# FFN inputs of a two-layer diffusion backbone: scale and shift of the turned tiles in one pass from PSUM, split between ScalarE and VectorE, and the column blocks' sums all on VectorE

## The chip, the cores and the metric

The kernel runs on one core of one Trainium2 chip. The metric is the device time of one execution in microseconds (us); the time given is the median of three runs. The engines are called TensorE (PE in the profile; PEld are its weight loads), VectorE (DVE), ScalarE (ACT), GpSimd (POOL) and SyncE (SP, which issues the DMAs). Each engine works through its own queue in order. TensorE writes its results to PSUM; in this kernel VectorE and ScalarE read them from there, and GpSimd works on SBUF alone.

## The reference

512 latent tokens and 256 context tokens with 1024 features pass through two layers. Each layer has a mixer and then a SwiGLU FFN; the input of each is normalised and modulated. What matters here is the FFN's input and its two first projections:

```python
def rms_norm(x, g):
    xf = x.astype(jnp.float32)
    y = xf * lax.rsqrt(jnp.mean(xf * xf, -1, keepdims=True) + NORM_EPS)
    return (y * g.astype(jnp.float32)).astype(x.dtype)

def modulate(h, shift, scale):
    return h * (1.0 + scale) + shift

def swiglu(u, w_gate, w_up, w_down):
    return (jax.nn.silu(u @ w_gate) * (u @ w_up)) @ w_down

# in each layer, behind the mixer's output y (and yc, the context's, in the first layer):
h = h + gt_m * rms_norm(y, g_post_mix[i])
f = swiglu(modulate(rms_norm(h, g_pre_ffn[i]), sh_f, sc_f), w_ffn_gate[i], w_ffn_up[i], w_ffn_down[i])
```

In the first layer all 768 tokens go through the FFN, in the second only the 512 latent ones. The FFN is 2816 wide.

## The kernel before

**Precision.** Every product of fp32 matrices is made of three products of halves: a value is split into a high part (ScalarE, `hi`) and a rest (`lo`, the value minus its high part, made by VectorE unless the call names GpSimd). This is the helper `split`, lines 179 to 182, so its instructions all bear lines 181 and 182 and are told apart by their tiles. TensorE then does high by high, high by rest and rest by high (`mm3`, lines 196 to 199).

**The output projection and what follows it** (`out_proj`, line 1403). A tile is 128 tokens: six in the first layer, worked on in the order 0 to 5, four in the second, in the order 0, 2, 1, 3. For each tile TensorE makes the second half of the projection (lines 1410 to 1412). ScalarE squares it for the norm (`junk`, line 1451), GpSimd makes the reciprocal root from the sums (`rr`, lines 221 and 228), and VectorE adds the result to the stream (lines 1536 to 1539 in the first layer, 2255 to 2258 in the second). Then `norm_W` (line 1505) prepares the FFN's input: ScalarE squares the new row (line 337), GpSimd makes `rr` again, ScalarE scales the row (`hn`, line 1508). TensorE turns the tile, four 128x128 blocks for each half of the 1024 features, into one of two PSUM banks (`ptp`, line 1513). In the turned tile the features lie on the partitions, so the norm's gain times (1 + scale) and the shift are one number per partition and block of features (`acol`, `scol`). VectorE multiplies the 128x512 half by its gains (line 1516), into the tile `nt`; the shift is added in a second pass (line 1517), by GpSimd for the first half of the features and by VectorE for the second. `Lagged(1)` puts one tile's second part behind the next tile's first part.

**The seven blocks.** The gate and up projections use Strassen's scheme in Winograd's form: a pair of token tiles makes the two columns of a 2x2 block matrix, the halves of the features its two rows, and seven products take the place of eight. `Winograd.add` (line 1485) makes the columns' seven blocks of each pair from the four `nt` halves. An even tile's halves are blocks 0 and 4 as they are. With an odd tile come four differences: block 1 (line 1492), block 2 (line 1497), block 3 (line 1499) and block 6 (line 1502), and block 5 is the tile's second half itself. Each block is split into `ub0` and `ub1` (both called `ub` in the profile) by `put`. Lines 1492 and 1499 are on GpSimd, except for the last tile, where they are on VectorE; line 1502 and the rest of block 5 (line 1501) are on GpSimd; the others are on VectorE.

**The FFN's first products** (`gate_up`, line 1566). For each pair of blocks of the weights and each of the two weight matrices, seven weight blocks meet the seven column blocks. Each product takes one block index of all pairs at once, so block 0 must be there for every pair before the first product can run through. The first two products use the blocks 0 and 4, the next ones 1, 5, 2, 3 and 6. The weights' own sums (`s`, lines 1603 to 1606) are made by GpSimd in the first layer; in the second layer three of four are made by VectorE. The sums of the products (lines 1609 to 1614) are on VectorE, the gate's activation on ScalarE, and the product of gate and up on GpSimd (line 1662).

**What sets the order.** The instructions of each engine are put in order by a planner before the launch, from the order in which the program issues them and from its own estimate of each instruction's time. The program issues a tile's preparation before the FFN's weights, but the planner lets weight work go ahead when it holds that the tile isn't ready.

Of the kernel before, what the change touches and what calls it, by code (L numbers as in the profile page):

```python
# [154 lines left out]
AF = mybir.ActivationFunctionType  # L155
ALU = mybir.AluOpType
# [7 lines left out]
def emit(tc, A):  # L164
    nc = tc.nc
    V, S, G, T = nc.vector, nc.scalar, nc.gpsimd, nc.tensor
# [8 lines left out]
    def bc(ap, n):  # L175

        return ap.unsqueeze(len(ap.shape)).to_broadcast(list(ap.shape) + [n])

    def split(hi, lo, src, lo_eng=None):

        S.activation(hi, src, AF.Copy)  # L181
        (lo_eng or V).tensor_tensor(lo, src, hi.bitcast(F32), ALU.subtract)  # L182
# [36 lines left out]
    def rsqrt_(out, ss, add):  # L219

        G.tensor_scalar(out, ss, add, None, ALU.add)
        n = 1
        for s in out.shape[1:]:
            n *= s
        nh = nhalf[:, :n]
        if len(out.shape) == 3:
            nh = nh.rearrange("p (a b) -> p a b", a=out.shape[1])
        G.tensor_tensor(out, out, nh, ALU.pow)
# [105 lines left out]
    def rstd_of(src, junk):  # L334
        ss = sm.tile([128, 1], F32, tag="ss", name="ss")
        r = sm.tile([128, 1], F32, tag="rr", name="rr")
        S.activation(junk, src, AF.Square, scale=1.0 / 32.0, accum_out=ss)
        rsqrt_(r, ss, EPS)
        return r

    def norm_T(src, a_col, s_col, pst, hi_out, lo_out):

        hn = tmpp.tile([128, 1024], F32, tag="hn", name="hn", bufs=2)
        r = rstd_of(src, hn)
        S.activation(hn, src, AF.Copy, scale=r)
        yield
        for hf in range(2):
            ps = pst()
            for k in range(4):
                T.transpose(ps[:, k * 128:(k + 1) * 128], hn[:, (hf * 4 + k) * 128:(hf * 4 + k + 1) * 128], ident)  # L350
            t = tmpp.tile([128, 4, 128], F32, tag="nt", name="nt", bufs=2)
            V.tensor_tensor(t, ps.rearrange("p (k t) -> p k t", k=4), bc(a_col[:, hf * 4:hf * 4 + 4], 128), ALU.mult)
            G.tensor_tensor(t, t, bc(s_col[:, hf * 4:hf * 4 + 4], 128), ALU.add)
            for (h, l, sv) in zip(hi_out(hf), lo_out(hf), split_view(t, len(hi_out(hf)))):
                split(h, l, sv)

    class Lagged:

# [4 lines left out]
        def add(self, gen):  # L363
            next(gen)
            self.q.append(gen)
            if len(self.q) > self.lag:
                self.pop()
# [22 lines left out]
    def split_view(t, n):  # L390
        if n == 1:
            return [t]
        v = t.rearrange("p k (r b c) -> p k r b c", r=2, b=8)
        return [v[:, :, i] for i in range(2)]
# [36 lines left out]
    def ptp(name="ptp"):  # L431
        return bank("v", name)
# [150 lines left out]
    def stile(nm):  # L583
        return gc.tile([128, 6, 16], F32, name=nm, tag=nm)

    av, gv, bv = stile("av"), stile("gv"), stile("bv")
    t0, t1, t2 = stile("t0"), stile("t1"), stile("t2")
# [26 lines left out]
    for d in range(2):  # L614
        rhs = gv[:, :, d * 8:(d + 1) * 8]
        ps = ptp("cum")
# [5 lines left out]
        ps = ptp("rest")  # L622
# [7 lines left out]
    for p in range(2):  # L630
        ps = ptp("tot")
# [828 lines left out]
    class Winograd:  # L1460
# [24 lines left out]
        def add(self, t, half_, x):  # L1485
            i = t // 2
            if t % 2 == 0:
                self.kept[i, half_] = x
                self.put(i, 4 * half_, x, V)
            elif half_ == 0:  # L1490
                b11 = self.kept[i, 0]
                (V if t == self.last else G).tensor_tensor(b11, x, b11, ALU.subtract)
                self.put(i, 1, b11, V)
                self.kept[i, 2] = x
            else:
                t1, b21, b12 = self.kept[i, 0], self.kept[i, 1], self.kept[i, 2]
                V.tensor_tensor(b12, x, b12, ALU.subtract)
                self.put(i, 2, b12, V)
                (V if t == self.last else G).tensor_tensor(t1, x, t1, ALU.subtract)
                self.put(i, 3, t1, V)  # L1500
                self.put(i, 5, x, G)
                G.tensor_tensor(b21, b21, t1, ALU.subtract)
                self.put(i, 6, b21, V)

    def norm_W(src, a_col, s_col, pst, U, t):
        hn = tmpp.tile([128, 1024], F32, tag="hn", name="hn", bufs=2)
        r = rstd_of(src, hn)
        S.activation(hn, src, AF.Copy, scale=r)
        yield
        for hf in range(2):  # L1510
            ps = pst()
            for k in range(4):
                U.turned = T.transpose(ps[:, k * 128:(k + 1) * 128], hn[:, (hf * 4 + k) * 128:(hf * 4 + k + 1) * 128], ident)
            x = tmpp.tile([128, 4, 128], F32, tag="nt", name="nt", bufs=6)
            ks = slice(hf * 4, hf * 4 + 4)
            V.tensor_tensor(x, ps.rearrange("p (k t) -> p k t", k=4), bc(a_col[:, ks], 128), ALU.mult)
            (V if hf else G).tensor_tensor(x, x, bc(s_col[:, ks], 128), ALU.add)
            U.add(t, hf, x)


# [10 lines left out]
    def post_mix0(t, ps, ss):  # L1531
        v = 0 if t < 4 else 1
        xt = tmpp.tile([128, 1024], F32, tag="xt", name="xt", bufs=2)
        nc.sync.dma_start(xt, A['x'][t * 128:(t + 1) * 128] if t < 4 else A['cx'][(t - 4) * 128:(t - 3) * 128])
        yt = tmpp.tile([128, 512], F32, tag="yt", name="yt")
        V.tensor_tensor(yt, ps, GG[v][:, 512:1024], ALU.mult)
        r = add_rstd(ss)
        V.scalar_tensor_tensor(xt[:, 0:512], U0.spare(t), r, xt[:, 0:512], ALU.mult, ALU.add)
        V.scalar_tensor_tensor(xt[:, 512:1024], yt, r, xt[:, 512:1024], ALU.mult, ALU.add)
        nc.sync.dma_start(h_d[t], xt)  # L1540
        yield from norm_W(xt, acol[v][:, 1, :], scol[v][:, 1, :], ptp, U0, t)
# [295 lines left out]
    def post_ffn0(t):  # L1837
        v = 0 if t < 4 else 1
        yield from norm_T(h[:, t, :], acol[v][:, 2, :], scol[v][:, 2, :], ptp, u_views(u1['h'], t), u_views(u1['l'], t))
# [413 lines left out]
    def post_mix1(t, ps, ss):  # L2253
        t2 = tmpp.tile([128, 512], F32, tag="yt", name="yt")
        V.tensor_tensor(t2, ps, GGs['m1'][0][:, 512:1024], ALU.mult)
        r = add_rstd(ss)
        V.scalar_tensor_tensor(h[:, t, 0:512], U1.spare(t), r, h[:, t, 0:512], ALU.mult, ALU.add)
        V.scalar_tensor_tensor(h[:, t, 512:1024], t2, r, h[:, t, 512:1024], ALU.mult, ALU.add)
        yield from norm_W(h[:, t, :], acol[0][:, 3, :], scol[0][:, 3, :], ptp, U1, t)
# [50 lines left out]
```

## Time and profile before

| | |
|---|---|
| median of three runs | 1999.85 us (1995.31 to 2003.21) |
| the profiled execution | 1996.12 us |
| its span in the profile | 1994.0 us |
| TensorE busy | 1830.4 us, 92% of the span |
| VectorE busy | 1436.1 us, 72% |
| ScalarE busy | 966.6 us, 48% |
| GpSimd busy | 928.0 us, 47% |
| granted TensorE clock, mean | 0.956 of full speed |

The profile comes from one execution. Its parts are the busy time of each engine, the span in 40 slices, the chain of work that ended last, and the groups of instructions by line, engine and tile with their count, busy time, mean duration and the idle time ahead of them. The trace can be asked the same of a stretch of time, and for the waits: which engine stood still at which line until which other engine's instruction had ended. A group's line reads: line, engine, operation, output<-inputs, shape, count; then busy us, mean ns; then the idle time before. Buffer numbers are left out of the names. A duration reaches from an instruction's start to its end; a queued instruction starts a little before its predecessor's end, so that durations in a row overlap slightly.

The changed lines run twice: from about 685 to 740 us (first layer) and from about 1607 to 1645 us (second layer).

### The profile page before, as it was taken

Reading aid. Unit: us, or ns where it says so; the run is one execution under the profiler, and the core shown is the slowest. Engines: PE = TensorE matmul, PEld = TensorE weight load, DVE = VectorE, ACT = ScalarE, POOL = GpSimd, SP = SyncE. Lnnn points to the kernel's source line nnn. Section 1 sums busy time; section 2 is a strip of 40 time slices with the busy share of each in tenths; the row PEclk is TensorE's granted clock in tenths of the full one; section 3 lists DMA queues with packets and bytes.
Section 4 is the critical chain, followed back from the end, with each engine's and each line's share of the span. In section 5 each row is a group of like instructions: output and inputs, shape, how many; then the busy total and the mean of one; then the engine's idle time right before and its main releaser. Section 6 shows DMA issues by size and latency. Waiting matters only on the chain.

```text
span 1994.0 us, 33781 instructions
## 1 busy us (share of the span) xinstructions
PE 1830.4 (92%) x12760; PEld 1504.2 (75%) x12760; DVE 1436.1 (72%) x2040; ACT 966.6 (48%) x1816; POOL 928.0 (47%) x828
## 2 busy tenths in 40 slices
PE   6989978989898979999999998889989959999998
PEld 3877855656566869999997776677655659999886
DVE  3686757677876696666656886887566589999654
ACT  4433457666874553333333345533455445445443
POOL 2387454344533376556547665653256142333101
PEclk7999978888999989999999999999999979999999
DMA  8255694665724613222227543586634212333221
GB/s 305 84 153 149 203 296 129 182 188 155 243 80 141 244 64 106 80 75 75 64 75 258 161 153 101 172 280 207 184 106 121 85 64 85 106 107 96 85 95 64
DMA packets 125751, 280.20 MB, mean 141 GB/s; under 512 B 12882, under 2 KB 43498, under 8 KB 125588
## 3 DMA queue, kind: packets, MB, share of 16 engines
q1 hardware_dynamic: 125588, 278.03, 44.0%
q8 instruction: 101, 1.65, 0.3%
q14 instruction: 62, 0.51, 0.1%
HBM read 226.15 MB, written 46.07 MB: 137 GB/s over the span
## 4 chain that ended last, share of the span: by engine, by line
PE 53%; DVE 9%; issue 4%; DMA 4%; POOL 3%; ACT 3%; SPq 0%; POOLq 0%; DVEq 0%; ACTq 0%
PE st L198 9%; PE st L199 9%; PE st L197 9%; PE dn L1696 4%; PE dn L1697 4%; PE dn L1698 4%; PE po L188 2%; DVE macc L254 2%; DMA mraw<-in_wmb_dram 2%; PE y L1410 1%; PE y L1411 1%; PE y L1412 1%; PE st L1958 1%; DVE ub L182 1%; PE st L1959 1%
## 5 line engine op out<-in xcount | busy, mean ns | idle before, releaser
L197 PE MATMUL st<-ub,hi_gu 128*128 128x384 f32 (+1 forms) x1232 | 385.8, 313 | 22.1 <-ACT ub L181 22.1
L198 PE MATMUL st<-ub,hi_gu 128*128 128x384 f32 (+1 forms) x1232 | 385.6, 313 | 1.1 <-DVE ub L182 1.0
L199 PE MATMUL st<-ub,lo_gu 128*128 128x384 f32 (+1 forms) x1232 | 384.3, 312 | 0.9 <-POOL lo_gu L182 0.9
L197 PEld LDWEIGHTS st<-ub,hi_gu 128*128 128x128 f32 x1232 | 233.9, 190 | 23.0 <-ACT ub L181 23.0
L199 PEld LDWEIGHTS st<-ub,lo_gu 128*128 128x128 f32 x1232 | 234.6, 190 | 1.6 <-POOL lo_gu L182 1.2
L198 PEld LDWEIGHTS st<-ub,hi_gu 128*128 128x128 f32 x1232 | 233.5, 190 | 2.0 <-DVE ub L182 2.0
L181 ACT ACTIVATE hi_gu<-s 128x512 fp32r<-128x512 f32 x176 | 111.1, 631 | 175.1 <-PE st L198 164.4
L1696 PE MATMUL dn<-hi_wd,gh 128*128 128x512 f32 x440 | 175.2, 398 | 2.2 <-ACT gh L181 2.2
L1697 PE MATMUL dn<-lo_wd,gh 128*128 128x512 f32 x440 | 175.0, 398 | 1.8 <-DVE lo_wd L182 1.8
L1698 PE MATMUL dn<-hi_wd,gl 128*128 128x512 f32 x440 | 165.3, 402 | 5.2 <-POOL gl L182 5.2
L182 DVE TENSOR_TENSOR lo_gu<-raw_gu,hi_gu 128x512 fp32r<-128x512 f32 x132 | 129.9, 998 | 42.8 <-ACT hi_gu L181 42.8
L182 DVE TENSOR_TENSOR lo_gu<-s,hi_gu 128x512 fp32r<-128x512 f32 x154 | 128.2, 833 | 45.1 <-ACT hi_gu L181 45.1
L254 DVE SCALAR_TENSOR_TENSOR macc<-mraw,cs,macc 128x1024 f32<-128x1024 f32 x80 | 125.5, 1592 | 22.8 <-DMA mraw<-in_wmb_dram 16.3
L181 ACT ACTIVATE hi_gu<-raw_gu 128x512 fp32r<-128x512 f32 x132 | 82.0, 629 | 98.8 <-PE st L198 91.9
L182 DVE TENSOR_TENSOR lo_wd<-raw_wd,hi_wd 128x512 fp32r<-128x512 f32 x110 | 96.8, 885 | 44.4 <-ACT hi_wd L181 44.3
L1606 POOL TENSOR_TENSOR s<-raw_gu 128x512 f32<-128x512 f32 x44 | 74.4, 1692 | 84.3 <-issue 70.7
L904 ACT ACTIVATE P<-st 128x512 f32<-128x512 f32 x128 | 73.0, 596 | 65.5 <-PE st L199 28.5
L1698 PEld LDWEIGHTS dn<-hi_wd,gl 128*128 128x128 f32 x440 | 82.3, 189 | 28.6 <-POOL gl L182 7.9
L1696 PEld LDWEIGHTS dn<-hi_wd,gh 128*128 128x128 f32 x440 | 83.0, 189 | 24.3 <-ACT gh L181 3.1
L181 ACT ACTIVATE gh<-g 128x512 fp32r<-128x512 f32 x76 | 47.5, 631 | 110.9 <-PE dn L1697 101.8
L1697 PEld LDWEIGHTS dn<-lo_wd,gh 128*128 128x128 f32 x440 | 83.0, 189 | 23.4 <-DVE lo_wd L182 2.7
L1662 POOL TENSOR_TENSOR g<-g,up 128x512 f32<-128x512 f32 x38 | 55.7, 1465 | 86.5 <-DVE up L1611 55.8
(545 smaller groups left out, 4794.7 us busy)
## 6 DMA issues: line engine op xcount, KB each, us to landing
mraw<-in_wmb_dram SPq DMA_DIRECT2D x56, 512.0 KB
raw_wd<-in_wd_dram SPq DMA_DIRECT2D x55, 512.0 KB
raw_gu<-in_wg_dram SPq DMA_DIRECT2D x44, 512.0 KB
raw_gu<-in_wu_dram SPq DMA_DIRECT2D x44, 512.0 KB
cu<-in_wmb_dram SPq DMA_DIRECT2D x24, 512.0 KB
raw_m<-in_wmb_dram SPq DMA_DIRECT2D x16, 512.0 KB
raw_qkv<-in_wqkv_dram SPq DMA_DIRECT2D x12, 512.0 KB
raw_tok<-qk_d SPq DMA_DIRECT2D x12, 512.0 KB
```

Of the source, the lines that this page charges most:

```text
L181: S.activation(hi, src, AF.Copy)
L182: (lo_eng or V).tensor_tensor(lo, src, hi.bitcast(F32), ALU.subtract)
L197: T.matmul(out, wh, xh, start=start, stop=False)
L198: T.matmul(out, wh, xl, start=False, stop=False)
L199: T.matmul(out, wl, xh, start=False, stop=stop)
L254: V.scalar_tensor_tensor(a, raw, cs[:, self.k, v:v + 1], a, ALU.mult, ALU.add)
L904: S.activation(P[:, :n], ps[:, :n], AF.Exp)
L1606: G.tensor_tensor(s3, a11, a21, ALU.subtract)
L1662: G.tensor_tensor(g, g, u, ALU.mult)
L1696: T.matmul(ps, gh[:, tsl], wh, start=start, stop=False)
L1697: T.matmul(ps, gh[:, tsl], wl, start=False, stop=False)
L1698: T.matmul(ps, gl_[:, tsl], wh, start=False, stop=stop)
```

## The change

The pass over a turned half tile becomes four smaller ones, one for each block of 128 features, each doing scale and shift at once from PSUM with the two numbers per partition as operands: by ScalarE for the first half of the features, by VectorE for the second. The separate shift falls away on both engines. The four instructions of `Winograd.add` that were on GpSimd (the differences for the blocks 1, 3 and 6, and the rest of block 5) go to VectorE.

```diff
+    def scaled(x, ps, a_col, s_col, hf):
+
+        for k in range(4):
+            a, b = [c[:, hf * 4 + k:hf * 4 + k + 1] for c in (a_col, s_col)]
+            if hf == 0:
+                S.activation(x[:, k, :], ps[:, k * 128:(k + 1) * 128], AF.Identity, scale=a, bias=b)
+            else:
+                V.tensor_scalar(x[:, k, :], ps[:, k * 128:(k + 1) * 128], a, b, ALU.mult, ALU.add)
...
@@ class Winograd, add
             elif half_ == 0:
                 b11 = self.kept[i, 0]
-                (V if t == self.last else G).tensor_tensor(b11, x, b11, ALU.subtract)
+                V.tensor_tensor(b11, x, b11, ALU.subtract)
                 self.put(i, 1, b11, V)
                 self.kept[i, 2] = x
             else:
                 t1, b21, b12 = self.kept[i, 0], self.kept[i, 1], self.kept[i, 2]
                 V.tensor_tensor(b12, x, b12, ALU.subtract)
                 self.put(i, 2, b12, V)
-                (V if t == self.last else G).tensor_tensor(t1, x, t1, ALU.subtract)
+                V.tensor_tensor(t1, x, t1, ALU.subtract)
                 self.put(i, 3, t1, V)
-                self.put(i, 5, x, G)
-                G.tensor_tensor(b21, b21, t1, ALU.subtract)
+                self.put(i, 5, x, V)
+                V.tensor_tensor(b21, b21, t1, ALU.subtract)
                 self.put(i, 6, b21, V)
...
@@ norm_W
             x = tmpp.tile([128, 4, 128], F32, tag="nt", name="nt", bufs=6)
-            ks = slice(hf * 4, hf * 4 + 4)
-            V.tensor_tensor(x, ps.rearrange("p (k t) -> p k t", k=4), bc(a_col[:, ks], 128), ALU.mult)
-            (V if hf else G).tensor_tensor(x, x, bc(s_col[:, ks], 128), ALU.add)
+            scaled(x, ps, a_col, s_col, hf)
             U.add(t, hf, x)
```

## The prediction

> **What bounds the kernel now.** The changed lines run in two short stretches, behind the output projections of the two layers, before their FFNs. I first asked what TensorE waits for there and afterwards. PE is TensorE, DVE VectorE, ACT ScalarE, POOL GpSimd; each wait row gives total us, times, longest. The waits of TensorE from 694 to 740 us (first layer, six token tiles):
>
> ```profile
> PE st L197 <- ACT ub L181: 5.6, 1, 5.6
> PE ptp L1513 <- DVE nt L1516: 4.3, 1, 4.3
> PE ptp L1513 <- ACT hn L1508: 3.0, 2, 2.2
> ```
>
> From 1607 to 1646 us (second layer, four tiles):
>
> ```profile
> PE st L197 <- ACT ub L181: 16.6, 2, 12.7
> PE ptp L1513 <- ACT hn L1508: 2.5, 1, 2.5
> ```
>
> From 740 to 1000 us, then from 1642 to 1860 us, the FFNs' products:
>
> ```profile
> PE st L199 <- POOL lo_gu L182: 0.9, 1, 0.9
> ```
>
> ```profile
> PE st L198 <- DVE ub L182: 1.0, 1, 1.0
> ```
>
> The reader is to see the contrast: some 13 and 19 us of waiting for the columns' blocks (ub) and the turned tiles, then next to none for hundreds of us. What brings TensorE back earlier is therefore handed on almost whole. The windows of both stretches tell which engine is full there (busy us and count of PE, PEld, DVE, ACT, POOL, then granted clock):
>
> ```profile
> 694.00:740.00 46.00, 33.06 (x164) 29.68 (x162) 44.20 (x50) 24.21 (x42) 34.20 (x29) 0.81 0.15 58
> 1607.00:1642.00 35.00, 14.90 (x89) 13.24 (x88) 34.41 (x43) 16.82 (x28) 20.96 (x21) 0.67 0.24 90
> ```
>
> TensorE is idle 46 - 33.1 = 12.9 and 35 - 14.9 = 20.1 us. VectorE is full, with 44.2 of 46 and 34.4 of 35; ScalarE is about half empty. Wherever the wait table says ACT ub, its input came through VectorE's queue. The bound is VectorE, and part of its time is not work. Its groups from 694 to 740 us (busy us, mean ns, idle before):
>
> ```profile
> L182 DVE TENSOR_TENSOR ub<-nt,ub 128x512 fp32r<-128x512 f32 x16 | 18.3, 1156 | 0.0
> L1517 DVE TENSOR_TENSOR nt<-nt,scol 128x512 f32<-128x512 f32 x5 | 4.8, 965 | 0.0
> L1538 DVE SCALAR_TENSOR_TENSOR xt<-ub,rr,xt 128x512 f32<-128x512 f32 x3 | 4.3, 1421 | 0.6 <-POOL rr L228 0.6
> L182 DVE TENSOR_TENSOR lo_gu<-s,hi_gu 128x512 fp32r<-128x512 f32 x3 | 3.1, 1044 | 0.0
> L1539 DVE SCALAR_TENSOR_TENSOR xt<-yt,rr,xt 128x512 f32<-128x512 f32 x3 | 3.0, 1002 | 0.0
> L1497 DVE TENSOR_TENSOR nt<-nt 128x512 f32<-128x512 f32 x3 | 2.1, 684 | 1.5 <-POOL nt L1492 1.5
> L1499 DVE TENSOR_TENSOR nt<-nt 128x512 f32<-128x512 f32 x1 | 1.7, 1670 | 0.0
> ```
>
> and from 1607 to 1642 us:
>
> ```profile
> L182 DVE TENSOR_TENSOR ub<-nt,ub 128x512 fp32r<-128x512 f32 x10 | 8.4, 838 | 0.1
> ...
> L1517 DVE TENSOR_TENSOR nt<-nt,scol 128x512 f32<-128x512 f32 x4 | 3.8, 951 | 0.0
> L1497 DVE TENSOR_TENSOR nt<-nt 128x512 f32<-128x512 f32 x2 | 3.4, 1708 | 0.0
> L2257 DVE SCALAR_TENSOR_TENSOR hbuf<-ub,rr,hbuf 128x512 f32<-128x512 f32 x2 | 3.3, 1639 | 0.1
> ...
> L1605 DVE TENSOR_TENSOR s<-raw_gu,s 128x512 f32<-128x512 f32 x2 | 2.4, 1210 | 0.0
> L182 DVE TENSOR_TENSOR lo_gu<-raw_gu,hi_gu 128x512 fp32r<-128x512 f32 x1 | 1.7, 1746 | 0.0
> ...
> L2258 DVE SCALAR_TENSOR_TENSOR hbuf<-yt,rr,hbuf 128x512 f32<-128x512 f32 x2 | 1.5, 738 | 0.0
> ```
>
> The same 512-column pass has a mean of 684 ns in one row (L1497, first stretch) and 1708 in another (second stretch). The long ones stand beside GpSimd. The timeline of VectorE, then of GpSimd, at 725 us (start, us):
>
> ```profile
> 724.94 0.68 DVE L1516 TENSOR_TENSOR nt<-ptp,acol 128x512 f32<-128x512 f32 x1
> 725.54 0.93 DVE L182 TENSOR_TENSOR ub<-nt,ub 128x512 fp32r<-128x512 f32 x1
> ```
>
> ```profile
> 724.50 1.42 POOL L1517 TENSOR_TENSOR nt<-nt,scol 128x512 f32<-128x512 f32 x1 [1.83 <-DVE nt L1516]
> ```
>
> While GpSimd's pass runs (to 725.92), VectorE's read from PSUM (ptp) keeps its 0.68; its next pass, with both tensors in SBUF, takes 0.93, and GpSimd itself needs 1.42.
>
> **The change part by part.** All that goes from GpSimd, and the scale that goes from VectorE, by the tile nt (ns min/median/max):
>
> ```profile
> L1516 DVE TENSOR_TENSOR nt<-ptp,acol x20: 674/678/692, 685.6 to 1635.7; 128x512 f32<-128x512 f32 x20
> ...
> L1517 POOL TENSOR_TENSOR nt<-nt,scol x10: 1038/1040/1485, 687.7 to 1636.0; 128x512 f32<-128x512 f32 x10
> ...
> L182 POOL TENSOR_TENSOR ub<-nt,ub x5: 1329/1592/1750, 699.0 to 1638.9; 128x512 fp32r<-128x512 f32 x5
> L1502 POOL TENSOR_TENSOR nt<-nt x5: 1286/1706/1743, 704.4 to 1643.1; 128x512 f32<-128x512 f32 x5
> L1492 POOL TENSOR_TENSOR nt<-nt x3: 1287/1615/1722, 697.2 to 1622.7; 128x512 f32<-128x512 f32 x3
> ```
>
> with another three of L1499: 10 shifts vanish and 5 + 5 + 3 + 3 = 16 passes move to VectorE. L1516 never exceeds 692 ns in 20 cases: a pass that reads PSUM is not stretched.
>
> The new instructions are 128x128 with two per-partition scalars, four per half tile. The nearest rows: VectorE's scale and shift of L509 (256 columns, from SBUF), plain copies of 128 columns out of PSUM on ScalarE (L1885, L1886), and ScalarE's 1024-column pass with a per-partition scale (L1508) beside one without (L337):
>
> ```profile
> 54.73 0.42 DVE L509 TENSOR_SCALAR ut<-hnT,acol,scol 128x256 f32<-128x256 f32 x1
> ...
> 55.66 1.06 DVE L509 TENSOR_SCALAR ut<-hnT,acol,scol 128x256 f32<-128x256 f32 x3
> ```
>
> ```profile
> 1345.13 0.29 ACT L1885 ACTIVATE gkt<-gkv 128x128 f32<-128x128 f32 x1
> 1345.29 0.30 ACT L1886 ACTIVATE gvt<-gkv 128x128 f32<-128x128 f32 x1
> ```
>
> ```profile
> L337 ACT ACTIVATE hn<-hbuf x10: 1056/1060/1063, 1229.7 to 1619.4; 128x1024 f32<-128x1024 f32 x10
> ...
> L1508 ACT ACTIVATE hn<-hbuf,rr x4: 1148/1152/1155, 1601.6 to 1621.5; 128x1024 f32<-128x1024 f32 x4
> ```
>
> *VectorE, second half of a tile.* Three in 1.06 us with 0.40 to 0.42 for one is a step of (1.06 - 0.40) / 2 = 0.33 us. Bounds for four: 0.68 (one L1516, no cost of splitting) and 4 x 0.42 = 1.7. I take 4 x 0.33 = 1.3, since L509 is the same operation. Out go the scale and the shift, 2 x 0.60 = 1.2 (a queued 0.68 pass is followed after 0.60: 724.94 to 725.54). Net +0.1 a tile.
> The Trainium skill, "VectorE: DVE Perf Modes", Rules for kernel authors, speaks against this part: a drain follows every operation, so keep the count of operations low. By that, each would pay its whole 0.42, 1.7 a tile, and the whole sum would be some 3.5 us worse over nine tiles. L509's 1.06 for three, under 3 x 0.42, says that part of it overlaps.
>
> *ScalarE, first half.* Copies start every 0.16 us; one per-partition scalar costs 1152 - 1060 = 92 ns. Bounds for four: 4 x 0.16 + 0.13 = 0.8 if the scalars are hidden (0.13 is what one copy's 0.29 has beyond its step), and 4 x (0.30 + 0.18) = 1.9. I take 4 x (0.16 + 0.18) + 0.13 = 1.5. It replaces 0.68 on VectorE plus 1.04 on GpSimd, so the first half is not later. Cover: ScalarE's 22 and 18 free us, against six and four times 1.5. Without it: behind the four wait the next tile's hn (L1508) and the hi parts (L181), since each engine works in order. I charge 1.5 once, for one hn that TensorE waits for.
> The Trainium skill, "ScalarE: Activation LUTs", What ACT_TABLE_LOAD costs, gives about 93 ns for each such operand and 93 ns of overlap; an estimate by it is 4 x 0.39 + 0.09 = 1.6 us. The 92 ns row agrees, and by the page the sum would be under 1 us worse.
>
> *VectorE, the sums.* Per pair of tiles: L1492, L1499, the lo of block 5, L1502. The last pair's first two were on VectorE already. First stretch: 4 + 4 + 2 = 10 passes x 0.60 = +6.0; second: 4 + 2 = 6 x 0.60 = +3.6. New wait: L1492 now waits for ScalarE's four, and L1497 and the second half may queue behind it; before, it waited for GpSimd's shift (and L1497 sat idle 1.5 behind it).
>
> *Work on VectorE, netted.* First stretch, tiles 1 to 5: -5 x 0.60 + 5 x 0.1 + 6.0 = +3.5. Second: -4 x 0.60 + 4 x 0.1 + 3.6 = +1.6. By count the change makes VectorE's queue longer.
>
> *The stretching that goes.* Measured against 0.68, and against 0.74 (L2258) for the three-input passes L1538, L1539 and L2257. First stretch: 16 x 0.48 + 5 x 0.29 + 3 x 0.68 + 3 x 0.36 + 3 x 0.26 + 0.99 = 14 us. GpSimd keeps some partners, each good for about 1.07 (1.75 - 0.68). In the first stretch, the sums of the weights and one lo:
>
> ```profile
> L1604 POOL TENSOR_TENSOR s<-s,raw_gu 128x512 f32<-128x512 f32 x1 | 1.7, 1684 | 2.4 <-DVE lo_gu L182 2.4
> L1606 POOL TENSOR_TENSOR s<-raw_gu 128x512 f32<-128x512 f32 x1 | 1.3, 1295 | 0.6 <-DVE lo_gu L182 0.6
> ```
>
> four in all, 4.3 us that stay. Gone: 14 - 4.3 + 1.5 idle = 11.2. Second: 10 x 0.16 + 4 x 0.27 + 2 x 1.03 + 2 x 0.90 + 2 x 0.53 + 1.07 = 8.7, of which two L1606 keep 2.1:
>
> ```profile
> L1606 POOL TENSOR_TENSOR s<-raw_gu 128x512 f32<-128x512 f32 x2 | 3.1, 1531 | 0.0
> ```
>
> Gone: 6.6.
>
> **Sum:** (3.5 - 11.2) + (1.6 - 6.6) + 1.5 = -11.2 us. What is late next: in the first stretch the hn of the last tile; in the second still VectorE. The rest of TensorE's 33 idle us remains. Against the profiled execution's 1996.1 (span 1994.0 and 2.1 around it) that is 1984.9. It lay 3.7 below the median of the three runs; from the median it would be 1988.7. I say 1986, a little nearer to the former, so that no change is about 1997. A measurement of this kernel can tell about 0.5%, 10 us, from no change.
>
> **The rivals.**
> *A better order (-16 to -22 us, 1975 to 1981).* VectorE's queue is laid out by a planner, which put weight sums and lo parts between the last tile's turning and its scale; ScalarE can take the first half at once. For: the 12.7 us wait hangs on that tile. Against: its subtraction still goes through VectorE's queue. Price: half of that wait, 6, on top of the sum, and up to 11 if nearly all of it goes.
> *Taken back (0 to -7 us, about 1993.5).* The FFN starts with no slack on the weights' side: the first stretch is followed by that 0.9 us wait for GpSimd's lo_gu. If weights or their sums don't come earlier, the first stretch's 7.7 us are spent waiting there and the second leaves 5.0 - 1.5 = 3.5. For: zero slack. Against: GpSimd, which makes those sums, loses 26 passes, and the weights' buffers come free through VectorE's own lo passes, which come earlier too.
> *Slower (+10.5 us or more, 2007.5).* The long passes stay long, since the partner is whatever GpSimd does at that moment, its small rr steps included, and the sixteen moved passes meet it. Then only the netted work counts, +5.1, and each moved pass that runs long adds 1.07; from five of them on it is over 0.5% (5.1 + 5 x 1.07 = 10.5). For: GpSimd keeps weight sums in the first stretch. Against: the second stretch leaves only two there.
>
> **How the numbers follow.** The forecast (-8 to -16) has 0.48, the better order 0.12, taken back 0.32, slower 0.08. Of the forecast's 0.48 about 0.06 lies under 10 us. Faster by over 0.5%: 0.12 + 0.42 = 0.54; within: 0.32 + 0.06 = 0.38; slower: 0.08. Unknown prices move the sum by nine times +0.4 or -0.6 (VectorE's four) and by up to 2 (ScalarE's). The range goes from 1976, most of the better order, to 1998, a full taking back and a little noise; outside are the slower case and the tails.
>
> **What would show it.** GpSimd without nt and ub in both stretches; VectorE's ub passes near 0.68 in the second and still some at 1.7 in the first; the four at 0.33 on VectorE and 0.35 on ScalarE; TensorE's idle time in the second stretch down from 20 to about 14 us, in the first from 13 to about 7. It is wrong if VectorE stays full for as long as before, if TensorE's waits after 740 us grow by what was won, or if waits for ScalarE's hn take the place of those for ub.

## The result and the profile after

The changed kernel's median is 1979.3 us (four runs, 1973.9 to 1986.8), beside 2001.5 (1995.3 to 2003.4) for four runs of the kernel before. The ratio is 0.9914, with a 95% interval of 0.9888 to 0.9940, so about 17 us are gained. (The two medians alone lie 22 us apart; four executions of each scatter over 8 and 13 us, and the stretches below and the second comparison agree with the 17.) In a second comparison the changed kernel had 1980.1 us and a ratio of 0.9915 (0.9894 to 0.9937). The forecast of 1986 had the sign and the mechanism, but the gain is half as large again as its sum of 11.2 us.

The profiled execution of after took 1981.1 us (span 1979.3). I measure each stretch from the first product of the second half of the output projection (y<-wo_h) to the first of the FFN's down projection (dn<-hi_wd,gh). Their starts in after, by line and tile (ns min/median/max, first and last start); the second stretch's starts, 1577.7 and 1846.9, come from the same rows for the second layer alone:

```profile
L1419 PE MATMUL y<-wo_h,ub x80: 387/389/477, 660.8 to 1599.7; 128*128 128x512 f32 x80
```

```profile
L1703 PE MATMUL dn<-hi_wd,gh x440: 392/396/796, 1037.1 to 1969.6; 128*128 128x512 f32 x147
```

| us | before | after | difference |
|---|---|---|---|
| start to the first stretch | 665.2 | 660.8 | -4.4 |
| first stretch | 386.6 | 376.3 | -10.3 |
| from there to the second stretch | 534.8 | 540.6 | +5.8 |
| second stretch | 275.0 | 269.2 | -5.8 |

The stretches give -16.1 us, nearly all of the ratio's 17. The other two rows are taken up in the experiments.

TensorE's waits in after, first from 690 to 740 us (what it waits for: total us, times, longest):

```profile
PE st L197 <- ACT ub L181: 3.4, 1, 3.4
PE ptp L1522 <- ACT nt L362: 2.1, 1, 2.1
PE ptp L1522 <- ACT hn L1517: 0.4, 1, 0.4
PE ptp L1522 <- DVE nt L364: 0.3, 1, 0.3
```

From 1595 to 1640 us:

```profile
PE st L197 <- ACT ub L181: 7.4, 2, 6.1
PE ptp L1522 <- ACT hn L1517: 5.1, 2, 4.5
PE st L198 <- DVE ub L182: 1.2, 1, 1.2
```

Together 6.2 us where there were 12.9, and 13.7 where there were 19 to 20. The wait for ub in the second stretch fell from 16.6 to 7.4; a wait of 5.1 for ScalarE's hn took a part of its place (2.5 before). From 740 to 1000 us TensorE shows no wait at all, so the FFN hands on what is won.

The same work on both sides lies between the stretch's first product and the end of the last lo part of the columns' blocks (ub, L182). That is 665.2 to 740 and 1586.6 to 1646.2 us in before (busy us and count of PE, PEld, DVE, ACT, POOL, then granted clock):

```profile
665.20:740.00 74.80, 61.86 (x299) 53.69 (x298) 63.77 (x77) 38.88 (x72) 48.51 (x53) 0.89 0.31 111
1586.60:1646.20 59.60, 39.50 (x199) 34.30 (x198) 44.46 (x58) 24.94 (x46) 25.18 (x30) 0.77 0.19 71
```

and 660.8 to 724.9 and 1577.7 to 1630.6 us in after:

```profile
660.80:724.90 64.10, 57.82 (x289) 50.52 (x288) 54.47 (x93) 45.05 (x95) 26.23 (x37) 0.95 0.38 134
1577.70:1630.60 52.90, 39.21 (x194) 33.82 (x193) 37.70 (x67) 30.24 (x62) 11.29 (x20) 0.82 0.23 80
```

The rest (lo) of the last block is ready 10.7 and 6.7 us earlier. VectorE runs more instructions than before, 93 for 77 and 67 for 58, and is busy for 9.3 and 6.8 us less. So the time went out of the passes, not out of their number.

Its groups in the first of these windows, before (busy us, mean ns, idle before):

```profile
L182 DVE TENSOR_TENSOR ub<-nt,ub 128x512 fp32r<-128x512 f32 x18 | 19.7, 1104 | 0.6 <-ACT ub L181 0.6
...
L1538 DVE SCALAR_TENSOR_TENSOR xt<-ub,rr,xt 128x512 f32<-128x512 f32 x6 | 7.3, 1214 | 3.0 <-POOL rr L228 3.0
L1517 DVE TENSOR_TENSOR nt<-nt,scol 128x512 f32<-128x512 f32 x6 | 5.5, 918 | 0.0
L1539 DVE SCALAR_TENSOR_TENSOR xt<-yt,rr,xt 128x512 f32<-128x512 f32 x6 | 5.2, 872 | 0.0
L182 DVE TENSOR_TENSOR lo_gu<-s,hi_gu 128x512 fp32r<-128x512 f32 x4 | 4.9, 1234 | 0.7 <-ACT hi_gu L181 0.7
...
L182 DVE TENSOR_TENSOR lo_gu<-raw_gu,hi_gu 128x512 fp32r<-128x512 f32 x5 | 4.1, 854 | 0.0
```

and after:

```profile
L182 DVE TENSOR_TENSOR ub<-nt,ub 128x512 fp32r<-128x512 f32 x21 | 14.3, 710 | 0.0
L364 DVE TENSOR_SCALAR nt<-ptp,acol,scol 128x128 f32<-128x128 f32 x24 | 8.1, 399 | 0.5 <-PE ptp L1522 0.5
L182 DVE TENSOR_TENSOR lo_gu<-s,hi_gu 128x512 fp32r<-128x512 f32 x4 | 4.9, 1234 | 0.7 <-ACT hi_gu L181 0.7
L1545 DVE SCALAR_TENSOR_TENSOR xt<-ub,rr,xt 128x512 f32<-128x512 f32 x6 | 4.5, 748 | 2.5 <-POOL rr L228 2.5
...
L182 DVE TENSOR_TENSOR lo_gu<-raw_gu,hi_gu 128x512 fp32r<-128x512 f32 x5 | 3.2, 682 | 0.0
L1508 DVE TENSOR_TENSOR nt<-nt 128x512 f32<-128x512 f32 x3 | 3.1, 1046 | 0.0
L1511 DVE TENSOR_TENSOR nt<-nt 128x512 f32<-128x512 f32 x3 | 2.9, 961 | 0.0
```

The blocks' lo parts went from a mean of 1104 to 710 ns, the first of the two additions to the stream (L1538, now L1545) from 1214 to 748. What stays long in after (lo_gu<-s, L1508, L1511) runs beside the weights' sums and one of their lo parts, which GpSimd still makes in the first layer. VectorE's timeline there:

```profile
717.65 1.78 DVE L1508 TENSOR_TENSOR nt<-nt 128x512 f32<-128x512 f32 x1
719.35 1.78 DVE L182 TENSOR_TENSOR lo_gu<-s,hi_gu 128x512 fp32r<-128x512 f32 x1
```

and GpSimd's:

```profile
717.14 1.74 POOL L182 TENSOR_TENSOR lo_gu<-s,hi_gu 128x512 fp32r<-128x512 f32 x1
718.96 1.62 POOL L1612 TENSOR_TENSOR s<-raw_gu,s 128x512 f32<-128x512 f32 x1
```

In the second stretch the blocks' passes come down to their short length. Before, then after:

```profile
L182 DVE TENSOR_TENSOR ub<-nt,ub 128x512 fp32r<-128x512 f32 x12 | 10.3, 857 | 0.8 <-ACT ub L181 0.7
...
L2257 DVE SCALAR_TENSOR_TENSOR hbuf<-ub,rr,hbuf 128x512 f32<-128x512 f32 x4 | 4.8, 1195 | 0.8 <-POOL rr L228 0.8
...
L1497 DVE TENSOR_TENSOR nt<-nt 128x512 f32<-128x512 f32 x2 | 3.4, 1708 | 0.0
```

```profile
L182 DVE TENSOR_TENSOR ub<-nt,ub 128x512 fp32r<-128x512 f32 x14 | 9.2, 681 | 0.0
...
L2264 DVE SCALAR_TENSOR_TENSOR hbuf<-ub,rr,hbuf 128x512 f32<-128x512 f32 x4 | 4.0, 1000 | 1.2 <-POOL rr L228 1.2
...
L1511 DVE TENSOR_TENSOR nt<-nt 128x512 f32<-128x512 f32 x2 | 2.1, 1058 | 0.0
```

The last block is a mark in VectorE's queue; it is not what TensorE waits for last. TensorE's last waits in the first stretch, before and after, with the idle time in brackets:

```profile
719.24 1.97 PE L1513 MATMUL ptp<-ident,hn 128*128 128x128 f32 x8 [0.81 <-ACT hn L1508]
```

```profile
707.28 1.97 PE L1522 MATMUL ptp<-ident,hn 128*128 128x128 f32 x8 [0.42 <-ACT hn L1517]
```

That is 54.0 and 46.5 us after the stretch's start, 7.5 earlier, for the last tile's hn. That hn hangs on VectorE too: VectorE's second addition for this tile (L1539, now L1546) ends at 714.37 and 703.23, 6.7 us earlier counted from the start. The whole first stretch in one window each, before and after, tells the rest:

```profile
665.20:1051.80 386.60, 371.72 (x2049) 362.90 (x2048) 262.57 (x356) 159.29 (x285) 232.30 (x195) 0.98 0.27 89
660.80:1037.10 376.30, 368.95 (x2050) 361.33 (x2048) 252.81 (x372) 166.09 (x309) 209.71 (x179) 0.99 0.28 91
```

TensorE is idle for 7.5 us less (14.9, then 7.4) and busy for 2.8 us less with the same products. Behind the last wait its products follow each other at steps of 0.73 down to 0.28 us until 724.6 in before and of 0.18 from then on; in after the 0.18 is reached at 710.2. The granted clock was 0.57 from 705 to 725 us in before and 0.83 from 695 to 715 in after. So I put some 3 of the 10.3 us down to products that ran at a lower granted clock around the waits. In the second stretch idle time falls by 6.4 us (21.2, then 14.8) and busy time is 0.6 longer.

The new instructions by the tile nt, and then four of them in a row on each engine:

```profile
L362 ACT ACTIVATE nt<-ptp,scol,acol x40: 438/457/478, 681.4 to 1620.6; 128x128 f32<-128x128 f32 x40
L364 DVE TENSOR_SCALAR nt<-ptp,acol,scol x40: 393/398/408, 681.6 to 1623.3; 128x128 f32<-128x128 f32 x40
```

```profile
1609.40 1.49 ACT L362 ACTIVATE nt<-ptp,scol,acol 128x128 f32<-128x128 f32 x4
```

```profile
1611.18 1.36 DVE L364 TENSOR_SCALAR nt<-ptp,acol,scol 128x128 f32<-128x128 f32 x4
```

A step is (1.36 - 0.40) / 3 = 0.32 us on VectorE and (1.49 - 0.46) / 3 = 0.34 on ScalarE.

### The profile page after: what moved, and what is told of

It is laid out like the page before. It is cut to its first block, busy times and chain, and to the rows that moved or that the text cites. A ratio compares the mean times of both kernels' runs of the same rounds, so it can differ in the third digit from the quotient of the medians.

```text
span 1979.3 us, 33806 instructions
## 1 busy us (share of the span) xinstructions
PE 1825.2 (92%) x12760; PEld 1503.0 (76%) x12760; DVE 1422.3 (72%) x2066; ACT 979.3 (49%) x1856; POOL 894.5 (45%) x802
## 4 chain that ended last, share of the span: by engine, by line
PE 55%; DVE 7%; issue 3%; ACT 3%; DMA 3%; POOL 3%; SPq 0%; POOLq 0%; DVEq 0%; ACTq 0%
PE st L198 9%; PE st L197 9%; PE st L199 9%; PE dn L1703 4%; PE dn L1704 4%; PE dn L1705 4%; PE po L188 2%; DVE macc L254 2%; DMA mraw<-in_wmb_dram 2%; PE y L1419 1%; PE y L1420 1%; PE y L1421 1%; PE st L1965 1%; PE st L1966 1%; DVE lo_wd L182 1%
## 5 line engine op out<-in xcount | busy, mean ns | idle before, releaser
L197 PE MATMUL st<-ub,hi_gu 128*128 128x384 f32 (+1 forms) x1232 | 385.5, 313 | 10.8 <-ACT ub L181 10.8
L182 DVE TENSOR_TENSOR lo_gu<-s,hi_gu 128x512 fp32r<-128x512 f32 x154 | 128.1, 833 | 44.4 <-ACT hi_gu L181 44.4
L182 DVE TENSOR_TENSOR lo_gu<-raw_gu,hi_gu 128x512 fp32r<-128x512 f32 x132 | 127.2, 977 | 43.0 <-ACT hi_gu L181 43.0
L182 DVE TENSOR_TENSOR lo_wd<-raw_wd,hi_wd 128x512 fp32r<-128x512 f32 x110 | 96.5, 883 | 43.2 <-ACT hi_wd L181 43.0
```

The costliest lines, as they stand in the source:

```text
L197: T.matmul(out, wh, xh, start=start, stop=False)
```

## The experiments

My theory: VectorE's queue up to the last block sets when the FFN starts (by the waits above, in the first stretch of before and after it is rather the queue up to the last tile's additions), and its passes with both inputs in SBUF are lengthened by GpSimd's passes that read SBUF; taking those away is the gain. The first rival: only the number of VectorE's passes matters, or the new order. The second: ScalarE's queue binds. All results together, with the stretches of the profiled execution (the difference to after is the ratio's distance from 0.9914, times 2000; most intervals are 3 to 6 us wide on either side):

| kernel | median us | ratio to before (95%) | to after | first stretch | second |
|---|---|---|---|---|---|
| before | | 1 | +17 | 386.6 | 275.0 |
| after | 1979.3 | 0.9914 (0.9888 to 0.9940) | 0 | 376.3 | 269.2 |
| e1, sums alone | 1991.7 | 0.9975 (0.9959 to 0.9991) | +12 | 383.1 | 271.7 |
| e2, one pass alone | 1985.0 | 0.9945 (0.9930 to 0.9960) | +6 | 379.3 | 270.0 |
| e4, GpSimd reads | 1993.0 | 0.9988 (0.9975 to 1.0001) | +15 | 384.2 | 274.9 |
| e5, GpSimd writes | 1986.3 | 0.9953 (0.9935 to 0.9971) | +8 | 379.6 | 269.2 |
| e3, all on VectorE | 1989.6 | 0.9961 (0.9940 to 0.9981) | +9 | 382.9 | 272.2 |
| e6, all on ScalarE | 1988.4 | 0.9949 (0.9930 to 0.9968) | +7 | 384.7 | 269.4 |
| e8, six on ScalarE | 1981.8 | 0.9928 (0.9900 to 0.9956) | +3 | 379.7 | 269.3 |
| e7, weights on VectorE | 1981.2 | 0.9916 (0.9884 to 0.9949) | 0 | 378.3 | 267.5 |
| e11, one sum on VectorE | 1983.6 | 0.9941 (0.9920 to 0.9963) | +5 | 376.3 | 269.3 |
| e9, before again | 1998.5 | 1.0004 (0.9988 to 1.0019) | +18 | 386.8 | 275.5 |
| e10, after again | 1980.1 | 0.9915 (0.9894 to 0.9937) | 0 | 376.3 | 269.3 |

**One part alone.** e1 is the kernel before with all of the blocks' sums on VectorE and the scale and shift as they were. e2 has the one-pass scale and shift, with the sums where they were.

```diff
# e1: norm_W, against after
-            scaled(x, ps, a_col, s_col, hf)
+            ks = slice(hf * 4, hf * 4 + 4)
+            V.tensor_tensor(x, ps.rearrange("p (k t) -> p k t", k=4), bc(a_col[:, ks], 128), ALU.mult)
+            (V if hf else G).tensor_tensor(x, x, bc(s_col[:, ks], 128), ALU.add)
# e2: Winograd.add, against after
-                V.tensor_tensor(b11, x, b11, ALU.subtract)
+                (V if t == self.last else G).tensor_tensor(b11, x, b11, ALU.subtract)
...
-                V.tensor_tensor(t1, x, t1, ALU.subtract)
+                (V if t == self.last else G).tensor_tensor(t1, x, t1, ALU.subtract)
...
-                self.put(i, 5, x, V)
-                V.tensor_tensor(b21, b21, t1, ALU.subtract)
+                self.put(i, 5, x, G)
+                G.tensor_tensor(b21, b21, t1, ALU.subtract)
```

> Only the four sums move to VectorE; scale and shift stay as before (scale on VectorE, shift on GpSimd for the first half). The stretch theory (VectorE's passes over two SBUF tensors take 1.7 us instead of 0.68 while GpSimd works, and this is what the change removes): VectorE gets 16 passes of 0.60 more, and loses only the stretching by the 16 passes that leave, not that by the ten shifts. First stretch +6.0 - 5.9, second +3.6 - 2.3: about +1.4 us on before, so no measurable change; TensorE's first-stretch length (first product of the second projection half to the first down product) near 387 us, the second near 276. The count theory (passes are passes, the gain of the change came from scale and shift in one): +9.6 us. If the sums alone are the gain: 10 us or more below before.

> Only scale and shift in one pass from PSUM (first half on ScalarE, second on VectorE); the sums stay where they were, on GpSimd. The stretch theory: VectorE loses 9 scale passes net of 0.1 each for the four small ones (-2.5 and -2.0 us), and the stretching by nine shifts of 1.07 each (-5.3 and -4.3), against 1.5 for ScalarE's four: about -12.6 us on before, so most of the change's gain; GpSimd's sums still stretch passes to 1.7. The count theory: -4.5 us, as VectorE's own count tells, and with e1 at +9.6 the two parts would add up to a slower kernel, which the change is not.

Both are faster than before: e1 by 5 us (3.5 and 3.3 in its stretches), e2 by 11 (7.3 and 5.0), near the 12.6 expected. e1 is the telling one. It puts eleven and five instructions more into VectorE's queue ahead of the last block (88 for 77, 63 for 58), and still the last block is ready 3.1 and 4.2 us earlier. So the count is not what decides, and this half of the first rival falls; the new order is left to e4. My own expectation for e1, 1.4 us slower, was off as well: its lo parts came down from 1104 to 762 ns although ten shifts stayed on GpSimd. Together the two parts give 16 us, about what the whole change gives; in the stretches they give 10.8 and 8.3 beside 10.3 and 5.8, so in the second they overlap.

**GpSimd's passes put back, with and without reading.** In e4, GpSimd also makes, for each odd tile, four sums of two tiles in SBUF that nobody uses, each behind a copy of one element that ties it to its place in time. In e5 each sum is replaced by two memsets, which read nothing.

```diff
# e4, after each of the puts of blocks 1, 3, 5 and 6
+        def idle(self, i, b):
+            hi, lo = [u[:, i, b].bitcast(F32) for u in self.hl]
+            j = tmpp.tile([128, 4, 128], F32, tag="idle", name="idle", bufs=1)
+            G.tensor_copy(j[0:1, 0, 0:1], lo[0:1, 0, 0:1])
+            G.tensor_tensor(j, hi, lo, ALU.add)
# e5, in place of the last line
+            G.memset(j, 0.0)
+            G.memset(j, 1.0)
```

> The changed kernel plus 20 passes of 128x512 on GpSimd (12 in the first stretch, 8 in the second), each reading two SBUF tiles (a block's two parts) that VectorE has just finished, into a tile that nobody reads. Nobody waits for them but what stands behind them in GpSimd's queue. The stretch theory: VectorE's ub and nt passes have a mean near 1.1 us again in both stretches and TensorE's idle time grows; 8 to 15 us slower than the changed kernel. The count theory: VectorE's work is what it was, so 0 to 3 us, from the small root steps that queue behind them on GpSimd.

> As e4, but each GpSimd pass is a pair of memsets of 128x512 into the unread tile, about 2 x 0.53 us from the 1024-column memset of the profile, which occupies GpSimd's queue about as long and reads nothing. If any GpSimd work in SBUF stretches VectorE's passes: like e4, 6 to 12 us slower than the changed kernel. If only GpSimd work that reads SBUF does: VectorE's passes stay at 0.68 and the time is within 3 us of the changed kernel. The count theory expects the same of e4 and e5, both 0 to 3 us.

VectorE's row for the blocks in the first and the second stretch, up to the last block (windows as above). In e4:

```profile
L182 DVE TENSOR_TENSOR ub<-nt,ub 128x512 fp32r<-128x512 f32 x21 | 20.1, 986 | 0.0
...
L182 DVE TENSOR_TENSOR ub<-nt,ub 128x512 fp32r<-128x512 f32 x14 | 11.1, 827 | 0.0
```

In e5's first stretch (the row of its second is after's, 9.2 us and 681 ns):

```profile
L182 DVE TENSOR_TENSOR ub<-nt,ub 128x512 fp32r<-128x512 f32 x21 | 13.8, 686 | 2.9 <-ACT ub L181 2.9
```

e4's VectorE has the same instructions as after's, in the same order up to the last block, and is back at 986 and 827 ns; nearly the whole gain is gone, 15 of 17 us (+7.9 and +5.7 in the stretches). So it is not the new order either. Here TensorE waits for late blocks as well, up to 732.5 us in the first stretch. In the second only three of the eight sums lie ahead of the last block; 3.2 of its 5.7 us are waits behind it, for the lo parts of weights that VectorE makes. The memsets leave the passes at 686 and 681 ns, and e5's second stretch is after's to the tenth. So it is the reading that costs, not a busy GpSimd. The pairs are not of equal length (a mean of 1.49 us for the nine sums ahead of the first stretch's last block, twice 0.53 for the memsets). e5's first stretch is still 3.3 us longer. The extra wait there is 3.8 us of TensorE for hn: GpSimd's reciprocal root stood behind the added instructions (last section). By the ratio e5 lies 8 us above after, where at most 3 were expected; the part that the stretches don't show stays open. The Trainium skill, "SBUF — State Buffer", the section on the two separate sides of SBUF, says that VectorE with two SBUF inputs and GpSimd share one pair of ports as an exclusive lock, and only against an operation of GpSimd that reads SBUF. The runs agree: 986 ns against reading sums, 686 against memsets.

**Who does the small passes.** Four per tile on each engine in after; none, six and all eight on ScalarE in e3, e8 and e6.

```diff
-            if hf == 0:
+            if hf == 2:             # e3: all on VectorE
+            if hf == 0 or k < 2:    # e8: six on ScalarE
+            if hf < 2:              # e6: all on ScalarE
```

> The changed kernel with all eight small passes of a tile on VectorE, none on ScalarE. Theory (VectorE's queue up to the last block of columns sets when the FFN starts): VectorE gets four more small passes of 0.33 us per tile, 1.3 us; five or six tiles of the first stretch and four of the second lie ahead of the last block, so +7 to +8 and +4 to +5, in all +11 to +13 us against the changed kernel, about 1991; the blocks' passes stay near 0.68. Rival (ScalarE's queue, which is full early in both stretches, and the wait for hn bind): ScalarE is relieved of 1.4 us a tile, the hn waits of 4 to 5 us in the second stretch go, and the time stays within 4 us of the changed kernel.

> The changed kernel with six of a tile's eight small passes on ScalarE and two on VectorE. VectorE loses 0.66 us a tile, ScalarE gains 0.7. If VectorE's queue alone decides: -3 to -4 us in the first stretch and -2 to -3 in the second, about -6. If ScalarE already binds: 0 to +4. I expect about -2, since ScalarE is full only in the first third of each stretch.

> The changed kernel with all eight small passes of a tile on ScalarE. VectorE loses 1.3 us a tile, ScalarE gains 1.4. If VectorE's queue alone decides: -6 to -8 us in the first stretch and -4 to -5 in the second, near 1968. If ScalarE becomes the bound: up to the last block it is busy 45 of 64 us in the changed kernel's first stretch and 30 of 53 in the second, so it would have 53 and 36; it then is full from the first hn on, each tile's hn waits behind eight small passes of 2.8 us, and TensorE's waits for hn grow: 0 to +8 us. I expect the second, about +3.

From 700 to 720 us, windows of e3 and then of e6:

```profile
700.00:720.00 20.00, 14.73 (x69) 13.53 (x70) 20.00 (x43) 11.63 (x20) 4.61 (x4) 0.71 0.07 27
```

```profile
700.00:720.00 20.00, 9.81 (x36) 8.15 (x35) 13.49 (x22) 19.88 (x46) 2.86 (x6) 0.58 0.13 52
```

In e3 VectorE is full (20.00 of 20) and ScalarE has room; its stretches are 6.6 and 3.0 us longer, a little under the 7 to 8 and 4 to 5 expected. In e6 it is the other way round, ScalarE 19.88 and VectorE 13.49, and TensorE waits for hn, from 690 to 760 us:

```profile
PE ptp L1522 <- ACT hn L1517: 9.9, 2, 6.9
```

That costs 8.4 us in the first stretch, more than the 3 expected, and nothing in the second, where there are four tiles. e8 was expected at -2 and came out at +3, with 7.2 us of waits for hn in the first stretch. That e8's first stretch lost 3.4 us although its last block was not later (62.7 us after the start, 64.1 in after) fits the waits: the last of them ended 50.5 us after the start, 46.5 in after. Of the four splits tried, four and four was the fastest, though e8's interval overlaps with it.

**What GpSimd still reads.** e7 moves the weights' sums and the rest made by GpSimd for the first gate and up groups of each layer to VectorE, e11 only the last sum in the second layer.

```diff
# e7
-            adder = V if wide else G
+            adder = V if wide or f == 0 else G
...
-            G.tensor_tensor(s3, a11, a21, ALU.subtract)
+            (V if f == 0 else G).tensor_tensor(s3, a11, a21, ALU.subtract)
# e11, the last line alone
+            (V if wide and f == 0 else G).tensor_tensor(s3, a11, a21, ALU.subtract)
```

> The changed kernel with the sums of the weights and the one lo part that GpSimd still makes for the first gate and up groups moved to VectorE, so that GpSimd reads no large tile in either stretch. Theory (a pass of GpSimd that reads two tiles of SBUF costs VectorE about 1.07 us, the same pass done by VectorE 0.60): up to the last block of columns four or five such passes go in the first stretch and two in the second: 5 x 0.60 - 4.7 = -1.7 and 2 x 0.60 - 1.8 = -0.6, about -2 us; VectorE's blocks and lo parts all near 0.68. Rival (only the count of VectorE's passes matters): +3.0 and +1.2 up to the last block, and as much again for the second group, +4 to +8 us.

> The changed kernel with only the last sum of the weights of the second layer's first two groups moved from GpSimd to VectorE: two to three passes, which cost VectorE 1.07 us each when they meet one of its own and 0.60 when it does them itself. Theory: second stretch 269.2 down by 1 to 2 us (the kernel with all weights' sums moved showed 267.5 there), first stretch unchanged at 376 within 2. Rival (only VectorE's count of passes matters): up by 1.2 to 1.8.

e7 gives nothing: +2.0 and -1.7 in the stretches, where the theory had -1.7 and -0.6; the median is within 2 us of after's. Its VectorE passes are short everywhere (lo parts of the blocks 683 ns from 690 to 735 us), so the lengthening did go. But ten more passes stand ahead of the first stretch's last block (103 for 93), twice what I had expected: 6.0 us at 0.60 each, against 4.8 of lengthening that could go, and that block is ready 1.2 us later. e11's stretches are after's within a tenth, neither theory's number; its median is 4 to 5 us higher, with intervals that overlap. Two passes more against 1.8 us of lengthening make its second stretch's last block ready 0.5 us earlier (52.4 for 52.9 after the start), but TensorE's last wait there ends no earlier (49.2 for 49.1). Neither is a better version. In VectorE's queue a moved pass pays while it takes away more lengthening than the 0.60 us that it costs; that the kernel gains by it isn't shown for these last ones.

**Both kernels again.** Nothing edited.

> The kernel before, unchanged, profiled once more. The two first profiles differ by 4.4 us before the first stretch, where both kernels have the same instructions in the same order, and by 5.8 us the other way between the stretches. If both are differences from execution to execution: this run's part before the first stretch lies between 655 and 665 us, its part from the first layer's down products to the second stretch near 540 us as in six of the other kernels (534.8 in the first profile of before), and the stretches stay at 386 and 275 us within 2. If the change really gives 5.8 us back between the layers, this run shows 535 there again.

> The changed kernel, unchanged, profiled once more. If the differences outside of the stretches come from execution to execution: before the first stretch between 655 and 665 us, between the layers near 540; the stretches at 376 and 269 us within 2; ratio to before 0.991.

The first products started at 662.1 and 660.6 us, and from the first stretch to the second it took 540.3 and 540.5 us; the stretches were 386.8 and 275.5, 376.3 and 269.3. So the -4.4 and +5.8 us outside the stretches in the first pair of profiles belong to single executions, and the stretches repeat within 0.5 us. The split of the first stretch repeats as well: TensorE is idle for 7.5 us less and busy for 3.0 less; the 0.6 more of the second doesn't. By this pair the change is worth 10.5 + 6.2 = 16.7 us.

## Why the prediction was right, and where its size was off

The bound, the mechanism and the direction held. The term of the sum that was mis-sized is the stretching that goes, and the sum took VectorE's gain up to the last block for TensorE's, which waits for something earlier, and had no term for TensorE's clock. Term by term, the upper rows up to the last block, from the rows above:

| us | forecast, first | measured | forecast, second | measured |
|---|---|---|---|---|
| passes out and in, at 0.60 and the small ones at 0.33 | +3.5 | +3.1 | +1.6 | +1.1 |
| VectorE's stretching that goes | -9.7 | -12.0 | -6.6 | -7.6 |
| VectorE's idle time | -1.5 | -1.3 | | 0.0 |
| sum | -7.7 | -10.2 | -5.0 | -6.5 |
| last block ready | | -10.7 | | -6.7 |
| TensorE's idle time | about -6 | -7.5 | about -6 | -6.4 |
| TensorE's busy time, same products | none | -2.8 | none | +0.6 |
| FFN's first down product | | -10.3 | | -5.8 |

- **The stretching.** The forecast added it up from 694 and 1607 us on, 14 and 8.7 us. The stretches begin earlier. Counted from their first products it is 16.8 in the first (18 x 0.42 for ub, 6 x 0.47 for L1538, 4 x 0.55 for lo_gu<-s, 6 x 0.24 for L1517, 6 x 0.13 for L1539, 5 x 0.17 for lo_gu<-raw_gu, and one L1499 of 1.67, 1.0), and 9.4 in the second. What was to stay was right: 4.3 forecast and 4.8 found in the first (four lo_gu of 1234 ns, three L1508, three L1511 and little more), 2.1 and 1.8 in the second. The blocks' lo parts in the first were expected to show some of 1.7 us still; the longest is 1.32, and those of 1.78 are a subtraction (L1508) and a lo part of the weights.
- **The passes.** In the first stretch 18 passes of 0.60 go, 24 of 0.33 and ten of 0.60 come: +3.1. The forecast had left out the first tile, which loses work too. In the second 12 passes of 0.60 go, 16 of 0.33 and six of 0.60 come, and one of the weights' sums fewer stands ahead of the last block: +1.1.
- **The small passes.** 1.36 us for four on VectorE (1.3 taken), 1.49 to 1.51 on ScalarE (1.5 taken). The estimate of 1.7 from the rule of the Trainium skill, "VectorE: DVE Perf Modes", Rules for kernel authors, is contradicted by the 1.36: queued ones follow at 0.32. The estimate of 1.6 by the Trainium skill, "ScalarE: Activation LUTs", What ACT_TABLE_LOAD costs, was close.
- **ScalarE's charge of 1.5.** The runs don't price it by itself. TensorE's waits for hn went from 3.0 to 0.4 us in the first stretch, where a wait of 2.1 for ScalarE's nt is new, and from 2.5 to 5.1 in the second. The 17.4 us won at the last block lie close to the 16.1 that reach the FFN, but they aren't handed on from there: TensorE's last wait ends before that block is ready in both stretches of both kernels.
- **TensorE's clock.** The forecast's sum has no term for it. By the profiles it gave some 3 of the first stretch's 10.3 us. That the shorter waits brought the clock back earlier is read from these profiles (e4, where the first stretch's idle time is 5.7 us longer than in after, has 2.1 us more of busy time); no run changes the clock alone.
- **TensorE's idle time.** 20 to 13.7 (14 forecast) and 13 to 6.2 (7 forecast): these two readings, taken by the waits, were nearer than the sum.
- **The rivals.** *Taken back*, with 0.32 the largest rival, did not happen: no wait of TensorE from 740 to 1000 us, where 0.9 was, nor from 1633 to 1846. Its premise, no slack on the weights' side, was the wrong reading of one wait of 0.9 us. *Slower* didn't come either; e4 shows its mechanism: with twenty reading passes added on GpSimd, the changed kernel is at 0.9988 of before, with nearly its whole gain gone. *A better order* gives the right number, and the wait of 12.7 us that it named did halve, to 6.1, but not for its reason. From the last tile's turning to the subtraction that this wait hangs on (block 1, L1492, now L1501) it took VectorE 15.3 us before and 8.6 after. Passes for the weights and the first products still stand in between, eight before and seven after, which is 0.6 of these 6.6 us; the lengthening there fell from 5.9 to 0.75, which is 5.2. In the first stretch VectorE does the same nine lo parts of weights ahead of the last block in both kernels.
- **The starting point.** "No change is about 1997" held: before again had 1998.5, and its pooled runs beside it 1997.2.

## What to carry to other kernels

Before counting instructions on a full engine, compare one form's mean duration beside and away from another engine's work; where the same pass takes 0.68 and 1.7 us, moving the partner onto the full engine can shorten it. Add up such lengthening from the first instruction of the stretch, not from where the waits begin, and up to the instruction that the waiting engine hangs on. Then balance the new work over the engines that can read PSUM, and stop when a moved pass costs as much as the lengthening that it removes. A shorter wait of TensorE can be worth more than its length, as here, where the granted clock was low around it.

## What the hardware showed unexpectedly

The lengthening has a second side: VectorE's passes also hold GpSimd up, and over several of them. GpSimd in e5, from 703 us:

```profile
703.31 3.11 POOL L1521 COPY idle<-ub 1x1 f32<-1x1 f32 x1
706.48 0.52 POOL L1522 MEMSET idle<- 128x512 f32 x1
...
707.67 2.47 POOL L221 TENSOR_SCALAR rr<-ss 128x1 f32<-128x1 f32 x1
```

VectorE in the same microseconds:

```profile
703.18 0.73 DVE L1556 SCALAR_TENSOR_TENSOR xt<-ub,rr,xt 128x512 f32<-128x512 f32 x1
703.84 0.74 DVE L1557 SCALAR_TENSOR_TENSOR xt<-yt,rr,xt 128x512 f32<-128x512 f32 x1
704.50 0.67 DVE L1501 TENSOR_TENSOR nt<-nt 128x512 f32<-128x512 f32 x1
705.11 1.28 DVE L182 TENSOR_TENSOR ub<-nt,ub 128x512 fp32r<-128x512 f32 x2
706.31 1.35 DVE L364 TENSOR_SCALAR nt<-ptp,acol,scol 128x128 f32<-128x128 f32 x4
707.59 0.67 DVE L1507 TENSOR_TENSOR nt<-nt 128x512 f32<-128x512 f32 x1
```

A copy of one element, 0.17 us at its shortest, takes 3.11: it begins beside a row of five passes with two SBUF inputs and ends at 706.42, when VectorE has turned to PSUM (706.31). The two memsets behind it keep their 0.52. The reciprocal root's first step (rr<-ss, 0.22 at its shortest) then takes 2.47: it begins beside the next row of such passes and ends at 710.14, when that row is over (its last pass ends at 710.06). ScalarE stands idle for it:

```profile
710.83 1.15 ACT L1528 ACTIVATE hn<-xt,rr 128x1024 f32<-128x1024 f32 x1 [3.35 <-POOL rr L228]
```

The 3.35 in brackets is its wait for the root, and TensorE's 3.8 us for hn follow from it. So a small step on GpSimd in a chain that someone waits for can stand behind a whole row of VectorE's passes. In these two cases GpSimd came through when VectorE's next pass read PSUM and when its row ended; that the row was what held it is read from these times alone.
